# A feed-forward input made of seven products: PSUM evictions, weight buffers and adding DMAs rearranged

## The chip, the cores and the metric

The kernel runs on one core of one Trainium2 chip. The metric is the device time of one execution in microseconds; lower is better. The time before is the median of three runs.

## The reference, cut to what matters

The kernel computes one inference step of one decoder layer for 512 prompt tokens and 8 sampled tokens, 520 columns in all. Only the last part of the layer is touched: an RMSNorm, the feed-forward input (two projections of width 2816 from 1024), SwiGLU, and the projection back.

```python
    h = x + (m @ w_o).astype(x.dtype)

    hn = rms_norm(h, norm_ffn_g)
    f_gate, f_up = jnp.split(hn @ w_ffn_in, 2, axis=-1)
    h = h + ((jax.nn.silu(f_gate) * f_up) @ w_ffn_down).astype(x.dtype)
```

Every matrix product is wanted at float32 accuracy. The kernel splits each float32 operand into a high and a low float32r part and adds three products of parts (high x high, high x low, low x high).

## The kernel before

The layer is computed with features on the 128 partitions and the 520 tokens along the free dimension, in two halves of 260 columns, L and R. Stages follow each other in the program: retention heads, gMLP, the merge, the `w_o` projection (L826 to L835), and then the feed-forward part, which begins at about 778 us of the profiled execution. The program is written in the Tile layer: instructions are recorded in program order, and a planner (`schedule_with_timeline_sim=True`, L1012) orders them on each engine by program order and by modelled times of when their data and a free buffer are there. The hardware then works through each engine's queue in that order. GpSimd and SP also issue the DMAs, in their queues.

The feed-forward input has 22 output blocks of 128 gate columns and 128 up columns. One call of `ffn_in(i)` (a pair below) makes one such block for both halves of the tokens. Instead of eight block products (two halves of the contraction, gate and up, two halves of tokens) it uses seven, by sums in the manner of Strassen and Winograd. The names are those of the code:

- `sum_weights` (L727 to L755) makes the seven weight operands of a pair. `ab` are two plain blocks, loaded by SP (L743). `s13` is a pair of sums: SP loads one block twice (L740), and an adding DMA of GpSimd's queue adds two other blocks (L741). `s24` is made from `s13` and `ab` by two VectorE additions (L750, L751). Each of these three tiles of 128x1024 is split (`split`, L88 on ScalarE for the high part, L91 on VectorE for the low part). The seventh operand, d, is loaded by a GpSimd DMA that converts it into `wdh` (L746); ScalarE writes its negative into `wdl` (L747), and a second, adding GpSimd DMA makes that the low part (L748).
- `wtile` (L74 to L79) hands out the buffers. For `wraw` it goes round five (three in pool `wp`, two in `wq`), for `whi` and `wlo` four each. `weights`, which loads the other projections, uses the same buffers.
- `sum_acts` (L757 to L803) makes the seven operands from the normalised input once, from a tile `xsum`.
- `seven` (L805 to L822) runs the seven products in the order of `ORDER`, each of 12 matmuls of 260 columns. They add into three PSUM banks: a, s2, s3, d into bank 0, s1 and s4 into bank 1, b into bank 2. Banks 0 and 1 are one tile of the pool `psm` (two buffers), bank 2 is one of `aux` (four buffers). After each product `seen` reads what is wanted of the partial sum.
- `seen` in `ffn_in` (L855 to L876) does these evictions: L857 (a), L859 (b), L861 (s1), L863 (s2), L865 (s3), L867 (s4), then on GpSimd the product of both halves of `fa` with `rstd` (L870), Silu on ScalarE (L871), the product of the right halves on GpSimd (L872) and, after d, the product of the left half straight from bank 0 on VectorE (L874).

The pairs come in batches of 10, 8 and 4; after each batch a down projection (`ffn_down`, L890) uses 8, 8 and 6 of the finished blocks. The planner mixes matmuls of neighbouring pairs, and of the down projection with pairs.

Of the kernel before, what the change touches and what calls it, by code (L numbers as in the profile page):

```python
# [7 lines left out]
F32 = mybir.dt.float32  # L8
F32R = mybir.dt.float32r
# [4 lines left out]
P = 128  # L14
# [27 lines left out]
def step_kernel(ctx: ExitStack, tc: tile.TileContext, io):  # L42
# [35 lines left out]
    def wtile(kind, dt=F32R):  # L78

        pools = wpools[kind]  # L80
        pool = pools[wturn[kind] % len(pools)]
        wturn[kind] += 1
        return pool.tile([P, 8 * P], dt, name=kind, tag=kind, bufs=pools.count(pool))

    def split(hi, lo, src, hi_eng=None, lo_eng=None):

        if hi_eng is None:
            nc.scalar.copy(out=hi, in_=src)  # L88
        else:
            hi_eng.tensor_copy(out=hi, in_=src)  # L90
        (lo_eng or nc.vector).tensor_tensor(out=lo, in0=src, in1=hi.bitcast(F32), op=ALU.subtract)  # L91
# [53 lines left out]
    def row_rstd(out, ps, width):  # L145

        y, v, t = (stile(f"rr_{x}") for x in "yvt")
        for f in range(2):
            nc.vector.tensor_scalar(
                out=v[:, f * HT : (f + 1) * HT], in0=ps[f][:, 0:HT], scalar1=1.0 / width, scalar2=EPS,  # L150
                op0=ALU.mult, op1=ALU.add,
            )
        root = nc.scalar.activation(out=y, in_=v, func=AF.Abs_reciprocal_sqrt)
        nc.vector.scalar_tensor_tensor(out=t, in0=y, scalar=-0.5, in1=y, op0=ALU.mult, op1=ALU.mult)
        nc.vector.tensor_tensor(out=t, in0=t, in1=v, op=ALU.mult)
        nc.vector.scalar_tensor_tensor(out=out, in0=t, scalar=1.5, in1=y, op0=ALU.add, op1=ALU.mult)
        return root
# [561 lines left out]

    ORDER = "a b s1 s2 s3 s4 d".split()
    MEETS = dict(a=0, s1=1, b=2, d=6, s4=3, s3=4, s2=5)

    fp = ctx.enter_context(tc.tile_pool(name="fp", bufs=1))
# [1 line left out]
    def sum_weights(src):  # L727

        def block(t):
            return t.rearrange("p (a b) -> p a b", a=2)  # L730

        def both(t):
            hi, lo = wtile("whi"), wtile("wlo")
            split(hi, lo, t)
            hi, lo = block(hi), block(lo)
            return [(hi[:, i], lo[:, i]) for i in range(2)]

        s13 = block(wtile("wraw", F32))
        for i in range(2):
            nc.sync.dma_start(out=s13[:, i], in_=src[:, 0])  # L740
        nc.gpsimd.dma_start(out=s13, in_=src[:, 1:3], accum_op=ALU.add)  # L741
        ab = block(wtile("wraw", F32))
        nc.sync.dma_start(out=ab, in_=src[:, 2:4])  # L743
        dh = wq.tile([P, 4 * P], F32R, name="wdh")
        dl = wq.tile([P, 4 * P], F32R, name="wdl")
        nc.gpsimd.dma_start(out=dh, in_=src[:, 1])  # L746
        nc.scalar.activation(out=dl, in_=dh.bitcast(F32), func=AF.Copy, scale=-1.0)  # L747
        nc.gpsimd.dma_start(out=dl, in_=src[:, 1], accum_op=ALU.add)  # L748
        s24 = block(wtile("wraw", F32))
        nc.vector.tensor_tensor(out=s24[:, 0], in0=s13[:, 0], in1=ab[:, 0], op=ALU.add)  # L750
        nc.vector.tensor_tensor(out=s24[:, 1], in0=s24[:, 0], in1=ab[:, 1], op=ALU.add)  # L751
        w = {"d": (dh, dl)}
        for names, t in (("a b", ab), ("s1 s3", s13), ("s2 s4", s24)):
            w |= dict(zip(names.split(), both(t.rearrange("p a b -> p (a b)"))))
        return w  # L755

    def sum_acts(fill, name, pairs):  # L757

        out = [[] for _ in range(7)]
        more = None  # L760
        for j in range(pairs):
            x = fp.tile([P, 7, HT], F32, name="xsum", bufs=1)
            fill(j, x)
            tt, stt = nc.vector.tensor_tensor, nc.vector.scalar_tensor_tensor
            tt(out=x[:, 4], in0=x[:, 3], in1=x[:, 1], op=ALU.subtract)
            tt(out=x[:, 1], in0=x[:, 0], in1=x[:, 1], op=ALU.subtract)
            stt(out=x[:, 5], in0=x[:, 3], scalar=-1.0, in1=x[:, 1], op0=ALU.mult, op1=ALU.subtract)
            stt(out=x[:, 6], in0=x[:, 5], scalar=-1.0, in1=x[:, 2], op0=ALU.mult, op1=ALU.subtract)

            def slots(t):  # L770
                return t.rearrange("p a (b c) -> p (a b) c", b=2)

            h, l = slots(pair(f"{name}h{j}")), slots(pair(f"{name}l{j}"))
            split(h, l, x[:, 0:4])
            for i in range(4):
                out[i].append((h[:, i], l[:, i]))

            if j % 2 == 0:
                more = [slots(pair(f"{name}m{j}{i}")) for i in range(3)]
            at = [(6 * k + 3 * (j % 2) + i) for k in range(2) for i in range(3)]  # L780
            at = [(more[n // 4], n % 4) for n in at]
            for k in range(2):
                i = 0
                while i < 3:
                    t, n = at[3 * k + i]
                    m = 1
                    while i + m < 3 and at[3 * k + i + m][0] is t:
                        m += 1
                    src = x[:, 4 + i : 4 + i + m]
                    if k == 0:  # L790
                        nc.scalar.copy(out=t[:, n : n + m], in_=src)
                    else:
                        for ii in range(i, i + m):
                            th, nh = at[ii]
                            tl, nl = at[3 + ii]
                            nc.vector.tensor_tensor(
                                out=tl[:, nl], in0=x[:, 4 + ii], in1=th[:, nh].bitcast(F32), op=ALU.subtract
                            )
                    i += m
            for i in range(3):  # L800
                (th, nh), (tl, nl) = at[i], at[3 + i]
                out[4 + i].append((th[:, nh], tl[:, nl]))
        return out  # L803

    def seven(w, x, name, seen):  # L805

        ps = acc_psum(name)
        bank = [ps[:, 0, 0:HT], ps[:, 1, 0:HT], aux(f"{name}3")[:, 0:HT]]
        into = dict(a=0, b=2, s1=1, s2=0, s3=0, s4=1, d=0)
        begun = set()  # L810
        for s in ORDER:
            to = into[s]
            acts = x[MEETS[s]]
            for k, (xh, xl) in enumerate(acts):
                sl = slice(k * P, (k + 1) * P)
                for n, (ww, xx) in enumerate(((w[s][0], xh), (w[s][0], xl), (w[s][1], xh))):
                    nc.tensor.matmul(  # L817
                        bank[to], ww[:, sl], xx, start=to not in begun,
                        stop=k == len(acts) - 1 and n == 2, skip_group_check=True,
                    )  # L820
                    begun.add(to)
            seen(s, bank)  # L822

    hs = fp.tile([P, KT, T], F32, name="hs")
# [19 lines left out]
    hx = sum_acts(fill_h, "hx", KT // 2)  # L844


    rstd = const.tile([P, T], F32, name="rstd")
    act = []
    L, R = slice(0, HT), slice(HT, T)

    def ffn_in(i):

        a, b = ttile("fa"), ttile("fb")

        def seen(s, bank):  # L855
            if s == "a":
                nc.scalar.copy(out=a[:, L], in_=bank[0])  # L857
            elif s == "b":
                nc.vector.tensor_tensor(out=a[:, L], in0=a[:, L], in1=bank[2], op=ALU.add)  # L859
            elif s == "s1":  # L860
                nc.scalar.activation(out=b[:, R], in_=bank[1], func=AF.Copy, scale=-1.0)  # L861
            elif s == "s2":
                nc.scalar.copy(out=a[:, R], in_=bank[0])  # L863
            elif s == "s3":
                nc.vector.tensor_tensor(out=b[:, R], in0=b[:, R], in1=bank[0], op=ALU.subtract)  # L865
            elif s == "s4":
                nc.vector.tensor_tensor(out=a[:, R], in0=a[:, R], in1=bank[1], op=ALU.add)  # L867
                if i == 0:
                    row_rstd(rstd, row_sums(sq), D)
                nc.gpsimd.tensor_tensor(out=a, in0=a, in1=rstd, op=ALU.mult)  # L870
                nc.scalar.activation(out=a, in_=a, func=AF.Silu)  # L871
                nc.gpsimd.tensor_tensor(out=b[:, R], in0=a[:, R], in1=b[:, R], op=ALU.mult)  # L872
            else:
                nc.vector.scalar_tensor_tensor(  # L874
                    out=b[:, L], in0=bank[0], scalar=-1.0, in1=a[:, L], op0=ALU.mult, op1=ALU.mult
                )  # L876

        seven(sum_weights(io["w_ffn_in"][i].rearrange("p (s c) -> p s c", s=4)), hx, "ps_f", seen)
        pr = pair(f"act{i}")
        split(pr[:, 0, :], pr[:, 1, :], b)  # L880
        act.append(pr)
# [143 lines left out]
```

## Time and profile before

| | us |
|---|---|
| runs | 1202.44, 1203.23, 1206.78; median 1203.23 |
| profiled execution | 1210.7 |
| its span in the trace | 1209.0 |
| TensorE busy | 1137.1 (94%) |
| VectorE busy | 761.1 (63%) |
| ScalarE busy | 500.2 (41%) |
| GpSimd busy | 313.0 (26%) |

Durations and waits are taken from the one profiled execution. In the rows PE is TensorE, PEld its weight loads, DVE VectorE, ACT ScalarE, POOL GpSimd and SP the engine that issues most loads. An output is written as out<-in by the program's tile names, with buffer numbers left out, so `wraw` stands for the tiles of `s13`, `ab` and `s24` alike. PEclk is the granted TensorE clock as a share of full speed. A wait names the instruction that came last before it.

### The profile page before, as it was taken

Reading aid. Unit: us, or ns where it says so; the run is one execution under the profiler, and the core shown is the slowest. Engines: PE = TensorE matmul, PEld = TensorE weight load, DVE = VectorE, ACT = ScalarE, POOL = GpSimd, SP = SyncE. Lnnn points to the kernel's source line nnn. Section 1 sums busy time; section 2 is a strip of 40 time slices with the busy share of each in tenths; the row PEclk is TensorE's granted clock in tenths of the full one; section 3 lists DMA queues with packets and bytes.
Section 4 is the critical chain, followed back from the end, with each engine's and each line's share of the span. In section 5 each row is a group of like instructions: output and inputs, shape, how many; then the busy total and the mean of one; then the engine's idle time right before and its main releaser. Section 6 shows DMA issues by size and latency. Waiting matters only on the chain.

```text
span 1209.0 us, 21757 instructions
## 1 busy us (share of the span) xinstructions
PE 1137.1 (94%) x8978; PEld 1113.8 (92%) x8978; DVE 761.1 (63%) x1192; ACT 500.2 (41%) x790; POOL 313.0 (26%) x286
## 2 busy tenths in 40 slices
PE   7999999999999998999999999988889978899994
PEld 7998999999999998999999999988879978899893
DVE  7778647965886687466434476966655545565654
ACT  4365346443633554232323333654443234432442
POOL 7213201310140031003111222223324223333343
PEclk9999999999999999998998999998999989999998
DMA  7267237533843475222222225447655457554502
GB/s 266 90 224 262 98 122 259 195 123 111 297 158 121 149 275 165 88 80 71 88 88 71 88 88 158 106 116 171 154 161 148 100 136 162 161 147 99 149 28 70
DMA packets 57603, 170.60 MB, mean 141 GB/s; under 512 B 6768, under 2 KB 9216, under 8 KB 57496
## 3 DMA queue, kind: packets, MB, share of 16 engines
q1 hardware_dynamic: 40320, 118.76, 29.9%
q0 software_dynamic: 17184, 50.45, 16.1%
q8 instruction: 70, 1.15, 0.4%
q14 instruction: 29, 0.24, 0.1%
HBM read 148.09 MB, written 21.10 MB: 140 GB/s over the span
## 4 chain that ended last, share of the span: by engine, by line
PE 63%; DMA 14%; DVE 11%; issue 4%; ACT 4%; POOL 1%; DVEq 0%; SPq 0%; POOLq 0%; ACTq 0%
PE ps_f L817 10%; PE ps_fd L109 10%; PE ps_ro L109 8%; DMA wraw<-in_w_ffn_in 7%; PE ps_v L109 5%; PE ps_gu L109 4%; PE ps_ar L109 4%; PE ps_gm L109 4%; PE ps_ag L109 3%; DVE wlo L91 3%; PE k L109 3%; PE ps_gv L109 3%; PE ps_wo L109 3%; DMA wdh<-in_w_ffn_in 3%; DMA S<-in_st 2%
## 5 line engine op out<-in xcount | busy, mean ns | idle before, releaser
L88 ACT CAST whi<-wraw 128x1024 fp32r<-128x1024 f32 (+3 forms) x205 | 210.2, 1027 | 350.7 <-issue 75.8
L91 DVE TENSOR_TENSOR wlo<-wraw,whi 128x1024 fp32r<-128x1024 f32 (+3 forms) x205 | 293.3, 1433 | 75.1 <-ACT whi L88 68.2
L817 PE MATMUL ps_f<-hxh,whi 128*128 128x260 f32 x352 | 104.4, 299 | 28.4 <-DVE fb L874 19.1
L109 PE MATMUL ps_fd<-act,whi 128*128 128x260 f32 x704 | 113.5, 282 | 1.0 <-DVE fb L874 0.8
L817 PE MATMUL ps_f<-hxl,whi 128*128 128x260 f32 x352 | 103.2, 294 | 1.8 <-DVE hxl L91 1.8
L817 PE MATMUL ps_f<-hxh,wlo 128*128 128x260 f32 x352 | 102.0, 294 | 0.0
L817 PEld LDWEIGHTS ps_f<-hxh,whi 128*128 128x128 f32 x352 | 69.4, 198 | 32.1 <-DVE fb L874 21.0
L109 PEld LDWEIGHTS ps_fd<-act,whi 128*128 128x128 f32 x704 | 96.7, 188 | 1.5 <-DVE fb L874 1.0
L109 PE MATMUL ps_g<-xg,whi 128*128 128x260 f32 x512 | 82.4, 283 | 0.0
L109 PE MATMUL ps_ro<-gated,whi 128*128 128x260 f32 x512 | 82.3, 283 | 0.0
L109 PE MATMUL ps_v<-xg,whi 128*128 128x260 f32 x512 | 82.1, 282 | 0.0
L817 PEld LDWEIGHTS ps_f<-hxl,whi 128*128 128x128 f32 x352 | 70.3, 200 | 2.0 <-DVE hxl L91 2.0
L109 PE MATMUL ps_fd<-act,wlo 128*128 128x260 f32 x352 | 71.9, 283 | 0.0
L109 PEld LDWEIGHTS ps_ro<-gated,whi 128*128 128x128 f32 x512 | 70.5, 188 | 0.5
L817 PEld LDWEIGHTS ps_f<-hxh,wlo 128*128 128x128 f32 x352 | 69.8, 200 | 0.4 <-DVE wlo L91 0.4
L109 PEld LDWEIGHTS ps_v<-xg,whi 128*128 128x128 f32 x512 | 70.0, 188 | 0.0
L109 PEld LDWEIGHTS ps_g<-xg,whi 128*128 128x128 f32 x512 | 69.7, 188 | 0.0
L817 PE MATMUL ps_f<-hxm,whi 128*128 128x260 f32 x352 | 68.2, 291 | 0.2 <-ACT fb L861 0.2
L453 POOL DMA_DIRECT2D out_rss<-S x32 | 17.0, 532 | 191.7 <-DVE S L452 191.7
L451 ACT ACTIVATE kv<-qkb,vs 128x256 f32<-128x256 f32 x128 | 54.1, 498 | 26.3 <-DMA qkb<-qks 20.7
L817 PEld LDWEIGHTS ps_f<-hxm,whi 128*128 128x128 f32 x352 | 56.9, 197 | 0.4 <-ACT fb L861 0.4
L456 DVE SCALAR_TENSOR_TENSOR junk<-S,qkb 128x256 f32<-128x256 f32 x128 | 53.9, 421 | 2.3
(268 smaller groups left out, 2835.7 us busy)
## 6 DMA issues: line engine op xcount, KB each, us to landing
wraw<-in_w_in SPq DMA_DIRECT2D x78, 512.0 KB, 3.5
S<-in_st SPq DMA_DIRECT2D x32, 512.0 KB, 4.6
out_rss<-S POOLq DMA_DIRECT2D x32, 512.0 KB, 5.0
wraw<-in_w_ffn_in SPq DMA_DIRECT2D x44, 256.0 KB, 4.0
wraw<-in_w_ffn_in POOLq DMA_DIRECT2D x22, 512.0 KB, 6.3
wraw<-in_w_ffn_in SPq DMA_DIRECT2D x22, 512.0 KB, 5.1
qkb<-qks POOLq DMA_DIRECT2D x16, 512.0 KB, 5.2
wraw<-in_w_ret_o SPq DMA_DIRECT2D x16, 512.0 KB, 3.5
```

Of the source, the lines that this page charges most:

```text
L88: nc.scalar.copy(out=hi, in_=src)
L91: (lo_eng or nc.vector).tensor_tensor(out=lo, in0=src, in1=hi.bitcast(F32), op=ALU.subtract)
L109: nc.tensor.matmul((ps[f] if isinstance(ps, list) else ps[:, f])[:, 0:HT], a, x[:, k, f * HT : (f + 1) * HT], start=first and n == 0, stop ...
L451: nc.scalar.activation(out=kv[:, j, :], in_=kb, func=AF.Copy, scale=vs[:, j, b : b + 1])
L453: nc.gpsimd.dma_start(out=io["rss"][b, h].rearrange("p (j d) -> p j d", j=NC), in_=S)
L456: nc.vector.scalar_tensor_tensor(out=junk, in0=S[:, j, :], scalar=1.0, in1=qb, op0=ALU.mult, op1=ALU.mult, accum_out=os_[:, j, b : b + 1],)
L817: nc.tensor.matmul(bank[to], ww[:, sl], xx, start=to not in begun, stop=k == len(acts) - 1 and n == 2, skip_group_check=True,)
```

## The change

The order of products becomes a, s1, b, s2, s3, s4, d. Product b is added onto product a: ScalarE copies bank 0 into bank 2 after a, and b adds there without starting anew. Evictions: b's bank is multiplied by `rstd` on its way out (left half), GpSimd multiplies only the right half by `rstd`, d's bank is copied out negated by ScalarE, and one GpSimd product over both halves follows. `rstd` is made after product a of the first pair. Four matmuls that nobody reads (`ps_mark`) stand ahead of the pairs.

For the weights: `s13` has the three buffers of `wp`, `ab` the two of `wq`, `s24` and the new plain tile `d` one each. d is loaded by SP as float32 and split like the others, last in the pair; the two GpSimd DMAs for it and the negated copy are gone. `ab` and `s13` are split ahead of the two sums. The tile `xsum` becomes two tiles of the large pool, and the last three operands of each part are split one by one.

```diff
-    ORDER = "a b s1 s2 s3 s4 d".split()
+    ORDER = "a s1 b s2 s3 s4 d".split()
...
-        s13 = block(wtile("wraw", F32))
+        s13 = block(wp.tile([P, 8 * P], F32, name="s13", tag="wraw", bufs=3))
         for i in range(2):
             nc.sync.dma_start(out=s13[:, i], in_=src[:, 0])
         nc.gpsimd.dma_start(out=s13, in_=src[:, 1:3], accum_op=ALU.add)
-        ab = block(wtile("wraw", F32))
+        ab = block(wq.tile([P, 8 * P], F32, name="ab", tag="wraw", bufs=2))
         nc.sync.dma_start(out=ab, in_=src[:, 2:4])
-        dh = wq.tile([P, 4 * P], F32R, name="wdh")
-        dl = wq.tile([P, 4 * P], F32R, name="wdl")
-        nc.gpsimd.dma_start(out=dh, in_=src[:, 1])
-        nc.scalar.activation(out=dl, in_=dh.bitcast(F32), func=AF.Copy, scale=-1.0)
-        nc.gpsimd.dma_start(out=dl, in_=src[:, 1], accum_op=ALU.add)
-        s24 = block(wtile("wraw", F32))
+        d = fp.tile([P, 4 * P], F32, name="d", bufs=1)
+        nc.sync.dma_start(out=d, in_=src[:, 1])
+        w = dict(zip("a b".split(), both(ab.rearrange("p a b -> p (a b)"))))
+        w |= dict(zip("s1 s3".split(), both(s13.rearrange("p a b -> p (a b)"))))
+        s24 = block(fp.tile([P, 8 * P], F32, name="s24", bufs=1))
         nc.vector.tensor_tensor(out=s24[:, 0], in0=s13[:, 0], in1=ab[:, 0], op=ALU.add)
         nc.vector.tensor_tensor(out=s24[:, 1], in0=s24[:, 0], in1=ab[:, 1], op=ALU.add)
-        w = {"d": (dh, dl)}
-        for names, t in (("a b", ab), ("s1 s3", s13), ("s2 s4", s24)):
-            w |= dict(zip(names.split(), both(t.rearrange("p a b -> p (a b)"))))
+        w |= dict(zip("s2 s4".split(), both(s24.rearrange("p a b -> p (a b)"))))
+        w["d"] = tuple(wq.tile([P, 4 * P], F32R, name=f"wd{x}") for x in "hl")
+        split(*w["d"], d)
         return w
...
-            x = fp.tile([P, 7, HT], F32, name="xsum", bufs=1)
-            fill(j, x)
+            x0, x1 = (wide("xsum").rearrange("p a (b c) -> p (a b) c", b=2) for _ in range(2))
+            x = [x0[:, i] for i in range(4)] + [x1[:, i] for i in range(3)]
+            fill(j, x0)
...
             for i in range(3):
                 (th, nh), (tl, nl) = at[i], at[3 + i]
+                split(th[:, nh], tl[:, nl], x[4 + i])
                 out[4 + i].append((th[:, nh], tl[:, nl]))
...
-        begun = set()
+        begun = {2}
...
+            if s == "a":
+                nc.scalar.copy(out=bank[2], in_=bank[0])
             seen(s, bank)
...
+    for _ in range(4):
+        nc.tensor.matmul(aux("ps_mark")[:, 0:HT], ones_r, hx[0][0][0], start=True, stop=True)
...
             if s == "a":
-                nc.scalar.copy(out=a[:, L], in_=bank[0])
+                if i == 0:
+                    row_rstd(rstd, row_sums(sq), D)
             elif s == "b":
-                nc.vector.tensor_tensor(out=a[:, L], in0=a[:, L], in1=bank[2], op=ALU.add)
+                nc.vector.tensor_tensor(out=a[:, L], in0=bank[2], in1=rstd[:, L], op=ALU.mult)
...
                 nc.vector.tensor_tensor(out=a[:, R], in0=a[:, R], in1=bank[1], op=ALU.add)
-                if i == 0:
-                    row_rstd(rstd, row_sums(sq), D)
-                nc.gpsimd.tensor_tensor(out=a, in0=a, in1=rstd, op=ALU.mult)
+                nc.gpsimd.tensor_tensor(out=a[:, R], in0=a[:, R], in1=rstd[:, R], op=ALU.mult)
                 nc.scalar.activation(out=a, in_=a, func=AF.Silu)
-                nc.gpsimd.tensor_tensor(out=b[:, R], in0=a[:, R], in1=b[:, R], op=ALU.mult)
             else:
-                nc.vector.scalar_tensor_tensor(
-                    out=b[:, L], in0=bank[0], scalar=-1.0, in1=a[:, L], op0=ALU.mult, op1=ALU.mult
-                )
+                nc.scalar.activation(out=b[:, L], in_=bank[0], func=AF.Copy, scale=-1.0)
+                nc.gpsimd.tensor_tensor(out=b, in0=a, in1=b, op=ALU.mult)
```

## Rows read from the trace of the kernel before

**Rows 1.** The page, busy time, share of the span and instructions of each engine.

```profile
PE 1137.1 (94%) x8978; PEld 1113.8 (92%) x8978; DVE 761.1 (63%) x1192; ACT 500.2 (41%) x790; POOL 313.0 (26%) x286
```

**Rows 2.** Busy time by stretch: its bounds, length, then each engine's busy time (instructions).

```profile
core 0: us, PE busy (x) PEld busy (x) DVE busy (x) ACT busy (x) POOL busy (x), PEclk, DMA share, GB/s
778.00:1157.00 379.00, 339.01 (x2657) 332.93 (x2655) 219.86 (x265) 151.92 (x222) 121.84 (x119) 0.96 0.57 139
800.00:908.00 108.00, 90.00 (x689) 87.49 (x688) 64.04 (x80) 49.50 (x77) 37.89 (x41) 0.95 0.67 165
908.00:952.00 44.00, 44.00 (x371) 44.00 (x370) 23.60 (x24) 11.79 (x14) 16.46 (x14) 1.00 0.55 129
```

**Rows 3.** The chain that ended last, second down projection: start, us, what.

```profile
1066.99 40.15 PE ps_fd L109 x336
```

**Rows 4.** TensorE's waits, 778 to 1157 us: total us, times, longest.

```profile
PE ps_f L817 <- DVE fb L874: 19.1, 9, 3.6
PE ps_f L817 <- ACT fa L857: 8.0, 3, 4.1
PE ps_f L817 <- DVE fa L867: 7.9, 4, 3.5
```

**Rows 5.** Timeline, VectorE and TensorE at 881 us: start, us, what, [idle before <-releaser].

```profile
881.14 0.69 DVE L750 TENSOR_TENSOR wraw<-wraw 128x512 f32<-128x512 f32 x1 [5.37 <-DMA wraw<-in_w_ffn_in]
881.75 0.42 DVE L867 TENSOR_TENSOR fa<-fa,ps_f 128x260 f32<-128x260 f32 x1
...
882.22 0.51 PE L817 MATMUL ps_f<-hxm,wdh 128*128 128x260 f32 x2 [3.31 <-DVE fa L867]
```

**Rows 6.** Timeline, ScalarE and TensorE at 899 us.

```profile
899.30 0.63 ACT L747 ACTIVATE wdl<-wdh 128x512 fp32r<-128x512 f32 x1 [3.84 <-DMA wdh<-in_w_ffn_in]
899.84 1.03 ACT L88 CAST whi<-wraw 128x1024 fp32r<-128x1024 f32 x1
900.77 0.37 ACT L857 COPY fa<-ps_f 128x260 f32<-128x260 f32 x1
...
901.19 0.39 PE L817 MATMUL ps_f<-hxh,whi 128*128 128x260 f32 x1 [2.58 <-ACT fa L857]
```

**Rows 7.** Timeline, GpSimd at 830 us.

```profile
830.65 0.85 POOL L741 DMA_DIRECT2D wraw<-in_w_ffn_in  x1 [8.16 <-DMA wraw<-in_w_ffn_in]
831.22 1.59 POOL L870 TENSOR_TENSOR fa<-fa,rstd 128x520 f32<-128x520 f32 x1
```

**Rows 8.** Waits of the other engines, 778 to 1157 us: total us, times, longest.

```profile
POOL wraw L741 <- DMA wraw<-in_w_ffn_in: 76.4, 12, 18.9
...
DVE wraw L750 <- DMA wraw<-in_w_ffn_in: 38.0, 15, 5.4
...
ACT fa L871 <- POOL fa L870: 32.2, 14, 4.9
...
ACT wdl L747 <- DMA wdh<-in_w_ffn_in: 30.9, 13, 4.6
...
ACT fa L857 <- PE ps_f L817: 3.0, 4, 0.8
```

**Rows 9.** The page, DMA issues: count, KB each, median us to landing.

```profile
wraw<-in_w_ffn_in SPq DMA_DIRECT2D x44, 256.0 KB, 4.0
wraw<-in_w_ffn_in POOLq DMA_DIRECT2D x22, 512.0 KB, 6.3
...
wdh<-in_w_ffn_in POOLq DMA_DIRECT2D x22, 256.0 KB, 4.9
```

**Rows 10.** Instruction groups, shapes apart, 778 to 1157 us: busy us, mean ns | idle.

```profile
L870 POOL TENSOR_TENSOR fa<-fa,rstd 128x520 f32<-128x520 f32 x22 | 34.3, 1559 | 50.2 <-DVE fa L867 49.9
...
L750 DVE TENSOR_TENSOR wraw<-wraw 128x512 f32<-128x512 f32 x20 | 17.1, 855 | 38.1 <-DMA wraw<-in_w_ffn_in 38.0
...
L863 ACT COPY fa<-ps_f 128x260 f32<-128x260 f32 x22 | 8.3, 375 | 14.6 <-PE ps_f L817 14.5
```

**Rows 11.** Waits of SP's DMA queue, whole span: total us, times, longest.

```profile
SPq L740 <- DVE wlo L91: 141.4, 20, 13.1
```

More of the change, by code (lines that the diff above doesn't have):

```diff
@@ L761, in sum_acts @@
         for j in range(pairs):
-            x = fp.tile([P, 7, HT], F32, name="xsum", bufs=1)
-            fill(j, x)
+            x0, x1 = (wide("xsum").rearrange("p a (b c) -> p (a b) c", b=2) for _ in range(2))
+            x = [x0[:, i] for i in range(4)] + [x1[:, i] for i in range(3)]
+            fill(j, x0)
             tt, stt = nc.vector.tensor_tensor, nc.vector.scalar_tensor_tensor
[L765 to L768, printed above, removed]
+            tt(out=x[4], in0=x[3], in1=x[1], op=ALU.subtract)
+            tt(out=x[1], in0=x[0], in1=x[1], op=ALU.subtract)
+            stt(out=x[5], in0=x[3], scalar=-1.0, in1=x[1], op0=ALU.mult, op1=ALU.subtract)
+            stt(out=x[6], in0=x[5], scalar=-1.0, in1=x[2], op0=ALU.mult, op1=ALU.subtract)
             def slots(t):
@@ L773, in sum_acts @@
             h, l = slots(pair(f"{name}h{j}")), slots(pair(f"{name}l{j}"))
-            split(h, l, x[:, 0:4])
+            split(h, l, x0)
             for i in range(4):
@@ L779, in sum_acts @@
                 more = [slots(pair(f"{name}m{j}{i}")) for i in range(3)]
[L780 to L797, printed above, removed]
-                            )
-                    i += m
+            at = [(more[n // 4], n % 4) for n in (6 * k + 3 * (j % 2) + i for k in range(2) for i in range(3))]
             for i in range(3):
                 (th, nh), (tl, nl) = at[i], at[3 + i]
+                split(th[:, nh], tl[:, nl], x[4 + i])
                 out[4 + i].append((th[:, nh], tl[:, nl]))
@@ L867, in seen @@
                 nc.vector.tensor_tensor(out=a[:, R], in0=a[:, R], in1=bank[1], op=ALU.add)
-                if i == 0:
-                    row_rstd(rstd, row_sums(sq), D)
-                nc.gpsimd.tensor_tensor(out=a, in0=a, in1=rstd, op=ALU.mult)
+                nc.gpsimd.tensor_tensor(out=a[:, R], in0=a[:, R], in1=rstd[:, R], op=ALU.mult)
                 nc.scalar.activation(out=a, in_=a, func=AF.Silu)
-                nc.gpsimd.tensor_tensor(out=b[:, R], in0=a[:, R], in1=b[:, R], op=ALU.mult)
             else:
-                nc.vector.scalar_tensor_tensor(
-                    out=b[:, L], in0=bank[0], scalar=-1.0, in1=a[:, L], op0=ALU.mult, op1=ALU.mult
-                )
+                nc.scalar.activation(out=b[:, L], in_=bank[0], func=AF.Copy, scale=-1.0)
+                nc.gpsimd.tensor_tensor(out=b, in0=a, in1=b, op=ALU.mult)
         seven(sum_weights(io["w_ffn_in"][i].rearrange("p (s c) -> p s c", s=4)), hx, "ps_f", seen)
```

## The prediction

> **What bounds the kernel now.** I read the page first, then the busy time of stretches, then the waits of the stretch that loses time, and last the queues behind those waits. TensorE is busy 94% of the span [rows 1], so only time in which it stands or runs slowly can be won. The change touches the stage from the first `ps_f` matmul (778 us) to the last (1157 us) and the few microseconds before it. That stage holds 2657 matmuls in 379.0 us [rows 2]. What one costs when nothing is late is seen in a down projection inside it: 336 matmuls in 40.15 us, 0.1195 us each [rows 3]. So 2657 x 0.1195 = 317.5 us are work and 61.5 us are lost. The loss is in the pairs (a pair is one call of `ffn_in`), not in the down projections: 800 to 908 us, nearly all pairs, has 689 matmuls at a granted clock of 0.95, where 908 to 952, nearly all down projection, is busy throughout at 1.00 [rows 2].
>
> TensorE's own waits in the stage are mostly three: for `fb` (L874) 19.1 us, for `fa` (L857) 8.0, for `fa` (L867) 7.9 [rows 4], together 35.0. The smaller ones bring that to 39.2 us; the other 61.5 - 39.2 = 22.3 us are the lower clock after a wait and the small restarts, 0.57 us for each us waited.
>
> Those three lines are only evictions out of the banks, of about 0.4 us. What is to be seen is why they were late: each engine works through its queue in order, and the planner that wrote the queues (modelled times, L1012) put a weight step ahead of the eviction whose data had not come. VectorE stood 5.37 us at L750, the first sum of weight blocks, for a DMA; the eviction L867 is right behind it, and TensorE waited 3.31 us for that [rows 5]. I followed the 13 waits of 19.1 and 7.9 us: in 11 of them L750 is the late step, in two (0.5 us each) nothing is. ScalarE stood 3.84 us at L747, the negated copy of `wdh`, for its DMA; the copy L857 is behind it and TensorE waited 2.58 us [rows 6]; the three waits of 8.0 us are all of this kind. In two of the 11 GpSimd was late first: its adding DMA L741 stood 8.16 us for the plain loads, and the product with `rstd` (L870) behind it held Silu and then L874 [rows 7]. In total L750 waited 38.0 us for DMAs, L747 30.9, L741 76.4 [rows 8].
>
> **The change part by part.** *The d block (L744 to L748).* Gone are two DMA issues on GpSimd and L747's wait. The old load wrote straight into `wdh`, so it could not start before TensorE had left that buffer; the new one goes to a buffer of its own, on SP, and is split last in its pair. The nearest row for its landing is SP's 256 KB load, 4.0 us, against 4.9 for the old one [rows 9]; its buffer is free again after the split before it, about one pair earlier (84 x 0.1195 = 10.0 us). So I take the whole of this wait as gone: 8.0 x 1.57 = 12.6 us. Ends: 0 (the split waits as L747 did) and 12.6. It costs VectorE 22 subtractions of 128x512; a two-input one of that shape has a mean of 0.855 us, or 0.69 undisturbed [rows 5, 10], so 15 to 19 us more on an engine that is busy 219.9 of 379.0 us [rows 2]. I cost that at nothing; if the cover fails it shows as a later eviction, as below.
>
> *Buffers by kind.* `s13` gets three buffers, `ab` two, the sums and d one each, in place of five shared. Today SP waits 141.4 us in 20 waits for a split (L91) to free a buffer before it can load s13 [rows 11]. From that load to the sum is a chain of landing 4.0, issue on GpSimd 0.85, landing 6.3 [rows 7, 9]: 11 us, longer than the pair's 10.0. With three buffers the load of a pair may start once the pair three before it is summed, some 30 us ahead, and the split of ab and s13 no longer stands behind the sum. What goes is L750's part: 19.1 + 7.9 = 27.0, with its clock 27.0 x 1.57 = 42.4 us. I take 60% of it, 25.4 us. Two of the 11 waits (3.25 + 3.64 of 25.9 us) began on GpSimd, and L741 is still placed there by modelled landings; the rest I leave for the first pairs after a down projection. Ends: 0 and 42.4. Next late is then GpSimd's product behind L741.
>
> *Evictions.* The last bank is copied out by ScalarE at once, not multiplied by Silu's result, so the buffer that the next pairs wait for no longer needs GpSimd's product (1.56 us mean) and Silu after s4 [rows 10]. It is behind Silu in ScalarE's queue if the planner puts it so; ScalarE waited 32.2 us there for GpSimd [rows 8]. That gain lies inside the 25.4. ScalarE gets 22 copies of 0.38 us, 8 us on an engine busy 151.9 of 379.0 [rows 2, 10]. GpSimd's elements are the same: 520 and 260 become 260 and 520.
>
> *The new wait.* Product b now adds onto the copy of a in the third bank, so TensorE needs that copy after one product of cover (s1, 12 x 0.1195 = 1.43 us). Queued behind it are the pair's whole rest, since TensorE is in order. The copy takes 0.375 us [rows 10]; but today its counterpart L857 waited for TensorE in only 4 of 22 pairs [rows 8], so in 18 it stood behind something, mostly casts of 1.0 us [rows 6]. One cast ahead: 1.0 + 0.375 is within the cover. Two: 2.1 + 0.375 + 0.15 = 2.6, so 1.2 us a pair. Ends 0 and 22 x 1.2 = 26.4 us; I take 0.2 a pair, 4.4 us, nearer to the one cast that rows 6 shows.
>
> *The rest.* Four `ps_mark` matmuls: 4 x 0.12 = 0.5 us. The Trainium skill, PSUM — Partial Sum Buffer, Summary: rules for kernel authors, speaks against the third bank: a sum seeded by ScalarE should start from 0, as engine writes don't set the bits by which a matmul adds. By it these matmuls are what makes the addition hold, and the 0.5 us is its price; no run here shows the bits. `xsum` moves to two tiles of the large pool and six casts of summed inputs become twelve: at most 0.4 us each on the last block, against L750 gone from between its steps; I take 0. `rstd` is made at a of the first pair; its matmuls run early already.
>
> Sum: -12.6 - 25.4 + 4.4 + 0.5 = -33.1 us. Against the profiled execution's 1210.7 us that is 1177.6; its span is 1209.0, and the runs' median of 1203.2 gives 1170.1 us.
>
> **The rivals.** *GpSimd stays the blocker (0.20).* L741 is queued where the loads are modelled to land, and every product and Silu behind it waits; the 76.4 us of rows 8 speak for it, that most were idle time with no product behind speaks against. Only the d part is won: -12.6 + 4.9 = -7.7, 1195.5 us.
>
> *The wait only moves (0.12).* Single buffers for d and the sums hold SP's queue: a load of d that waits for a split keeps the next s13 behind it. Then both kinds of stall stay, less a little issue time on GpSimd, which is not on the path: gain about 5 us against the 4.9 added, 1203 us. The Trainium skill, DMA: Bandwidth & Descriptors, Issuing engines are not separate DMA queues, agrees with this case: a transfer moved to another engine's queue saves only the time to issue it. Its landing has rows of 4.0 against 4.9 us, so the d part would then be near 0.
>
> *Slower: the copy of a (0.12).* Two casts stand ahead of the copy in every pair, at the second step of TensorE's order: +26.4, and sums placed early again keep the 42.4. Then -12.6 + 26.4 + 0.5 = +14.3, 1217.5 us. It decides from about 2.9 us between the end of a and the end of its copy (1.43 of cover + 33/22): from there the whole gain is gone. The 18 of 22 late copies speak for it, the room on ScalarE (152 of 379 us) against.
>
> **How the numbers follow.** The forecast has 0.56, own range 1150 to 1188: below it only the whole 42.4 and no new wait (1203.2 - 55 = 1148). The range 1150 to 1206 takes in the first two rivals and leaves out the slower one and the lowest end, about 0.17. A measurement of this kernel tells 0.5%, 6 us, from no change. Faster is the forecast and the first rival, 0.76; same the second, 0.12; slower the third, 0.12.
>
> **What would show it.** Right: L750 and the d split wait under 10 us each for DMAs in the stage; SP's waits for s13 fall from 141 us; TensorE's waits from 39 to under 20 and the clock of 800 to 900 us at 0.98 or more. Wrong: ScalarE's copy into the third bank tops TensorE's waits (slower rival); Silu's wait for GpSimd stays near 32 us (first); the d split waits near 31 us (second).

## The result and the profile after

The changed kernel takes 1160.3 us (median of 4 runs, 1157.44 to 1161.14) against 1203.4 before: 0.9633 of the time, 95% interval 0.9608 to 0.9658, so 43.1 us faster by the medians, where 33.1 were forecast. The profiled executions are 1210.7 and 1161.1 us, their spans 1209.0 and 1159.4. Of that difference of 49.6 about 5 us are most likely not the change's: in before's profiled execution, which is itself 7 us longer than the median, the first `ps_f` matmul comes at 778 us, in that of after at 773. The lead is there already at the first matmul of the stage before `w_o` (`ps_gm`, 687 against 681 us; 677 to 682 in the other kernels below, whichever weight path they have). What the change touches shrank from 379 us [rows 2] to 333.

Line numbers of after: L741 is the adding DMA as before, L749 and L750 the two sums, L799 the products, L805 the copy of bank 0 into bank 2, L848 b's eviction, L854 s3's, L856 s4's, L857 the half product with `rstd`, L858 Silu, L860 the negated copy of d's bank, L861 the last product. The tiles that all were `wraw` are now `s` (s13 and s24), `ab` and `d`.

Busy time of each engine over the span, from the page of after (compare [rows 1]):

```profile
PE 1120.1 (97%) x8982; PEld 1098.7 (95%) x8982; DVE 763.2 (66%) x1192; ACT 507.7 (44%) x818; POOL 292.6 (25%) x242
```

Busy time by stretch of after, columns as in [rows 2]: the stage, steady pairs, the start of the stage, the rest of it.

```profile
773.00:1106.00 333.00, 325.27 (x2653) 320.97 (x2651) 222.29 (x264) 159.07 (x245) 98.69 (x77) 0.99 0.52 139
800.00:880.00 80.00, 79.81 (x662) 79.19 (x661) 59.19 (x76) 48.19 (x79) 26.06 (x20) 1.00 0.61 166
773.00:791.00 18.00, 14.76 (x96) 13.86 (x95) 12.90 (x22) 10.44 (x18) 0.00 (x0) 0.81 0.24 65
791.00:1106.00 315.00, 310.52 (x2560) 307.11 (x2558) 209.39 (x243) 148.62 (x228) 98.69 (x77) 1.00 0.54 143
```

Steady pairs now run TensorE 79.81 of 80 us at a granted clock of 1.00; before it was 90.0 of 108 at 0.95 [rows 2]. With 0.1195 us a matmul [rows 3], the stage holds 2653 x 0.1195 = 317.0 us of work and loses 16.0, where it lost 61.5. That is 45.5 us won inside the stage. Of the 16.0 left, 18.0 - 96 x 0.1195 = 6.5 are lost in the first 18 us, at a granted clock of 0.81, TensorE's first waits for the input operands (`hxh`, `hxl` below) among them; the other 315 us lose 9.1.

TensorE's waits of after in the stage: who waited for whom, total us, times, longest.

```profile
PE ps_f L799 <- DVE fb L854: 1.6, 3, 0.5
PE ps_f L799 <- ACT hxh L88: 1.5, 1, 1.5
PE ps_fd L109 <- DVE fd L882: 1.3, 1, 1.3
PE ps_f L799 <- DVE hxl L91: 0.8, 1, 0.8
...
PE ps_f L799 <- ACT ps_f L805: 0.4, 2, 0.2
```

The 19.1, 8.0 and 7.9 us of [rows 4] are gone, and the new wait, for the copy into the third bank (L805), is 0.4 us. All of TensorE's waits for pairs and down projections (`ps_f` and `ps_fd`, 765 to 1160 us, so with the last down projection) come to 8.1 us here and to 39.1 before; below, "TensorE's waits" is always this sum. The waits of the engines that had stood in the way, same stretch:

```profile
POOL s L741 <- DMA s<-in_w_ffn_in: 33.8, 4, 20.5
...
ACT fa L858 <- POOL fa L857: 15.7, 20, 1.9
...
DVE s L749 <- DMA s<-in_w_ffn_in: 8.5, 1, 8.5
...
DVE s L749 <- DMA ab<-in_w_ffn_in: 4.1, 1, 4.1
```

VectorE's sum waits twice for a DMA, 12.6 us in all, where it waited 38.0 us in 15 waits [rows 8]; both lie in down projections, at 907 and 1041 us, and only the second costs TensorE anything, the 1.3 us for `fd` L882 above. ScalarE waits for no DMA of d any more, where it had 30.9 us [rows 8]. SP's queue still waits for a split to free the buffer of s13, and GpSimd's adding DMA (L741) for SP's loads, but TensorE now loses next to nothing by it; SP's row over the whole span, beside [rows 11]:

```profile
SPq L740 <- DVE wlo L91: 91.6, 22, 12.4
```

The timeline of after in a steady pair (start, us, what, and in brackets any idle time before it) shows what became of [rows 5]: the sum and the eviction behind it follow without a gap.

```profile
833.46 0.69 DVE L749 TENSOR_TENSOR s<-s,ab 128x512 f32<-128x512 f32 x1
...
834.12 0.43 DVE L848 TENSOR_TENSOR fa<-ps_f,rstd 128x260 f32<-128x260 f32 x1
```

### The profile page after: what moved, and what is told of

Its sections match the earlier page's. It is cut to its first block, busy times and chain, and to the rows that moved or that the text cites. A ratio compares the mean times of both kernels' runs of the same rounds, so it can differ in the third digit from the quotient of the medians.

```text
span 1159.4 us, 21723 instructions
## 1 busy us (share of the span) xinstructions
PE 1120.1 (97%) x8982; PEld 1098.7 (95%) x8982; DVE 763.2 (66%) x1192; ACT 507.7 (44%) x818; POOL 292.6 (25%) x242
## 4 chain that ended last, share of the span: by engine, by line
PE 77%; DVE 9%; DMA 4%; ACT 4%; issue 2%; POOL 1%; DVEq 0%; SPq 0%; ACTq 0%; POOLq 0%
PE ps_f L799 14%; PE ps_fd L109 10%; PE ps_ro L109 8%; PE ps_v L109 8%; PE ps_g L109 6%; PE ps_gu L109 4%; PE ps_ar L109 4%; PE ps_gm L109 4%; PE ps_gv L109 4%; PE ps_ag L109 3%; PE q L109 3%; PE k L109 3%; DVE wlo L91 2%; PE ps_o L469 2%; ACT whi L88 2%
## 5 line engine op out<-in xcount | busy, mean ns | idle before, releaser
L88 ACT CAST whi<-wraw 128x1024 fp32r<-128x1024 f32 (+3 forms) x139 | 141.3, 1018 | 278.5 <-issue 67.1
L91 DVE TENSOR_TENSOR wlo<-wraw,whi 128x1024 fp32r<-128x1024 f32 (+3 forms) x139 | 192.2, 1384 | 37.8 <-ACT whi L88 35.7
L799 PE MATMUL ps_f<-hxh,whi 128*128 128x260 f32 x352 | 101.3, 289 | 4.6 <-DVE fb L854 1.6
L799 PE MATMUL ps_f<-hxl,whi 128*128 128x260 f32 x352 | 100.2, 285 | 0.8 <-DVE hxl L91 0.8
L799 PE MATMUL ps_f<-hxh,wlo 128*128 128x260 f32 x352 | 99.8, 285 | 0.6 <-DVE wlo L91 0.6
L799 PEld LDWEIGHTS ps_f<-hxh,whi 128*128 128x128 f32 x352 | 67.1, 191 | 7.2 <-DVE fb L854 2.2
L91 DVE TENSOR_TENSOR wlo<-s,whi 128x1024 fp32r<-128x1024 f32 x44 | 61.7, 1403 | 14.9 <-ACT whi L88 14.4
L799 PEld LDWEIGHTS ps_f<-hxl,whi 128*128 128x128 f32 x352 | 67.2, 191 | 1.1 <-DVE hxl L91 1.1
L799 PEld LDWEIGHTS ps_f<-hxh,wlo 128*128 128x128 f32 x352 | 67.0, 191 | 0.8 <-DVE wlo L91 0.8
L799 PE MATMUL ps_f<-hxm,whi 128*128 128x260 f32 x352 | 65.2, 282 | 0.3 <-ACT fa L852 0.3
L88 ACT CAST whi<-s 128x1024 fp32r<-128x1024 f32 x44 | 46.1, 1048 | 37.8 <-PE ps_fd L109 20.3
```

The source lines that it names most:

```text
L799: nc.tensor.matmul(bank[to], ww[:, sl], xx, start=to not in begun, stop=k == len(acts) - 1 and n == 2, skip_group_check=True,)
```

## The experiments

Two theories were set against each other. The first is that of the prediction: the evictions were late because weight steps stood ahead of them in the queues of VectorE and ScalarE and waited for DMAs, and the DMAs were late because their loads waited for a buffer. The rival: the gain comes from the evictions themselves (the third bank, the earlier release of bank 0). All kernels below compute the whole layer. Each was timed in turn with the kernel before on the same chip; ratios are to that.

### The weight path alone

before, with after's `sum_weights`. It needs after's `sum_acts` too: the pool of the old `xsum` has no room for the new tiles beside it. ORDER, the three banks and the evictions are before's.

> The kernel before with the new weight path alone (own buffers by kind, d by SP and split last, ab and s13 split ahead of the sums) and xsum in the large pool, which makes the room for it; order and evictions as before. Theory 1 (the loss was weight steps waiting for DMAs in front of evictions): most of the 43 us are here, about 1172 us (1165 to 1180), TensorE's waits in the stage under 15 us. Theory 2 (the loss was that a bank is freed only after GpSimd's product and Silu): little is here, about 1195 us (1188 to 1203), and TensorE still waits about 20 us for fb.

1165.3 us, 0.968 [0.9656, 0.9703]: 38.5 us of the gain are here. TensorE's waits fall from 39.1 to 13.3 us; its two longest rows for the products (L847 is s3's eviction here) are

```profile
PE ps_f L799 <- DVE fb L847: 4.9, 4, 3.5
...
PE ps_f L799 <- ACT whi L88: 2.1, 1, 2.1
```

None of before's three rows is left, though the evictions are before's. The first theory holds for most of the gain. The longest wait left is of another kind:

```profile
806.94 0.88 POOL L741 DMA_DIRECT2D s<-in_w_ffn_in  x1 [5.58 <-DMA s<-in_w_ffn_in]
...
808.61 0.62 ACT L88 CAST act<-fb 128x520 fp32r<-128x520 f32 x1 [5.28 <-POOL fb L854]
...
809.27 0.70 DVE L91 TENSOR_TENSOR act<-fb,act 128x520 fp32r<-128x520 f32 x1 [5.21 <-ACT act L88]
809.88 0.42 DVE L847 TENSOR_TENSOR fb<-fb,ps_f 128x260 f32<-128x260 f32 x1
...
810.36 0.39 PE L799 MATMUL ps_f<-hxh,whi 128*128 128x260 f32 x1 [3.48 <-DVE fb L847]
```

GpSimd stood 5.58 us at its adding DMA for the plain loads; a product of the pair before (L854) is behind it, the split of that product waits for it on ScalarE and then on VectorE, and the eviction stands behind the split.

### The evictions alone

after, with before's `sum_weights`: third bank, new order and new evictions on the old weight path.

> The changed kernel with the weight path of before (five shared buffers, two GpSimd DMAs for d, sums ahead of the splits); order, third bank and plain evictions stay changed. Theory 1: about 1198 us (1190 to 1206), the VectorE sum still waits near 38 us for DMAs. Theory 2: about 1168 us (1160 to 1178), the bank is free early whatever the weights do.

1201.2 us, 0.9985 [0.9965, 1.0006]: no change that can be told. The waits, of TensorE and of those in its way (L855 is s3's eviction here, L806 the copy into bank 2):

```profile
DVE wraw L750 <- DMA wraw<-in_w_ffn_in: 52.5, 17, 7.2
...
ACT wdl L747 <- DMA wdh<-in_w_ffn_in: 32.5, 20, 3.2
...
PE ps_f L800 <- DVE fb L855: 23.7, 11, 5.0
...
PE ps_f L800 <- ACT ps_f L806: 10.3, 10, 3.4
```

The sum and the negated copy stand as long as before, or longer, and TensorE's waits come to 40.2 us against 39.1. What is new is the last row: the copy into bank 2 is itself late, behind ScalarE's negated copy. So the rival falls as the cause of the gain.

### d as before, the rest as after

```diff
-        d = fp.tile([P, 4 * P], F32, name="d", bufs=1)
-        nc.sync.dma_start(out=d, in_=src[:, 1])
+        dh = wq.tile([P, 4 * P], F32R, name="wdh")
+        dl = wq.tile([P, 4 * P], F32R, name="wdl")
+        nc.gpsimd.dma_start(out=dh, in_=src[:, 1])
+        nc.scalar.activation(out=dl, in_=dh.bitcast(F32), func=AF.Copy, scale=-1.0)
+        nc.gpsimd.dma_start(out=dl, in_=src[:, 1], accum_op=ALU.add)
...
-        w["d"] = tuple(wq.tile([P, 4 * P], F32R, name=f"wd{x}") for x in "hl")
-        split(*w["d"], d)
+        w["d"] = (dh, dl)
```

> The changed kernel with d loaded as before: two GpSimd DMAs straight into the split buffers and the negated copy on ScalarE between them. Theory 1: ScalarE waits for d again, 8 to 13 us in the pairs and about 3 us where the first two loads are issued in the gMLP stage: 1174 us (1168 to 1179). Theory 2: the evictions no longer depend on it, 1162 us (1159 to 1166).

1196.3 us, 0.9925 [0.9901, 0.995]: the old d path alone gives back 36 us of the 43, some two and a half times what was expected. Its waits:

```profile
ACT wdl L747 <- DMA wdh<-in_w_ffn_in: 38.3, 20, 3.9
...
PE ps_f L801 <- ACT ps_f L807: 22.8, 10, 4.4
```

One of them in the timeline at 812 us:

```profile
811.75 0.63 ACT L747 ACTIVATE wdl<-wdh 128x512 fp32r<-128x512 f32 x1 [3.65 <-DMA wdh<-in_w_ffn_in]
812.29 0.37 ACT L807 COPY ps_f<-ps_f 128x260 f32<-128x260 f32 x1
...
812.71 0.39 PE L801 MATMUL ps_f<-hxh,whi 128*128 128x260 f32 x1 [3.97 <-ACT ps_f L807]
```

ScalarE stands 3.65 us for the DMA of d. The copy of bank 0 into bank 2 is right behind it, and now TensorE needs that copy for its next products: it stands 3.97 us. Eight waits make up 22.4 of that row's 22.8 us, and in all of them the copy is right behind L747. In before, the 30.9 us of L747's waits cost TensorE 8.0 us [rows 4, 8]; with the third bank 38.3 cost it 22.8.

### Shared buffers, the rest as after

```diff
-        s13 = block(wp.tile([P, 8 * P], F32, name="s13", tag="wraw", bufs=3))
+        s13 = block(wtile("wraw", F32))
...
-        ab = block(wq.tile([P, 8 * P], F32, name="ab", tag="wraw", bufs=2))
+        ab = block(wtile("wraw", F32))
...
-        s24 = block(fp.tile([P, 8 * P], F32, name="s24", bufs=1))
+        s24 = block(wtile("wraw", F32))
```

> The changed kernel with s13, ab and s24 taken from the five shared buffers as before; d by SP, splits ahead of the sums and evictions stay changed. Theory 1: the loads of s13 wait for a buffer again and the sum waits for the adding DMA: about 1183 us (1173 to 1195). Theory 2: 1162 us (1159 to 1167), with the sum's waits back but TensorE not held by them.

1193.3 us, 0.9904 [0.9883, 0.9924]: this alone gives back 33 us. The sum waits again, and TensorE with it:

```profile
DVE wraw L749 <- DMA wraw<-in_w_ffn_in: 48.1, 15, 6.9
...
PE ps_f L799 <- DVE fb L854: 25.0, 11, 5.7
```

At 825 us it is the pattern of [rows 5] once more: three weight steps of VectorE stand between the late data and the eviction.

```profile
824.75 0.69 DVE L749 TENSOR_TENSOR wraw<-wraw 128x512 f32<-128x512 f32 x1 [3.42 <-DMA wraw<-in_w_ffn_in]
...
825.48 0.69 DVE L750 TENSOR_TENSOR wraw<-wraw 128x512 f32<-128x512 f32 x1
826.08 0.68 DVE L91 TENSOR_TENSOR wdl<-d,wdh 128x512 fp32r<-128x512 f32 x1
...
826.68 0.42 DVE L854 TENSOR_TENSOR fb<-fb,ps_f 128x260 f32<-128x260 f32 x1
...
827.16 0.39 PE L799 MATMUL ps_f<-hxh,whi 128*128 128x260 f32 x1 [2.01 <-DVE fb L854]
```

So undoing either part costs nearly all of the gain. Two readings were open: on the old evictions the parts might add (each worth what the prediction gave it), or either stall alone might cover the other. Two kernels put one part alone on before.

### Own buffers alone, on before

before, with the three buffer lines above the other way round, and with after's `sum_acts` and after's order of splits; d and the evictions stay before's.

> The kernel before (its order, evictions and d path) with own buffers for s13, ab and s24, their splits ahead of the sums, and xsum in the large pool. Adding theory (the two stalls have prices of their own, as the prediction summed them): 1203 - 25 = 1178 us (1170 to 1185). Covering theory (a pair that is held by one stall gives the other's transfer time to land, so that either of them alone costs nearly as much as both): 1190 to 1203 us, with ScalarE's wait for d above the 31 us of before and TensorE's waits near 25 us.

1188.9 us, 0.9866 [0.9826, 0.9906]: 16 us, between the ranges of the two theories. TensorE's waits are 28.5 us. The rows that matter:

```profile
ACT wdl L747 <- DMA wdh<-in_w_ffn_in: 39.2, 18, 8.1
...
PE ps_f L801 <- ACT fa L841: 8.3, 5, 2.7
PE ps_f L801 <- ACT whi L88: 7.8, 5, 2.4
...
DVE s L752 <- DMA s<-in_w_ffn_in: 7.8, 1, 7.8
DVE s L752 <- DMA ab<-in_w_ffn_in: 5.8, 1, 5.8
```

The sum's stall is down to two waits, 13.6 us, both in down projections, as own buffers should do. But the stall of d, which had cost TensorE 8.0 us in before, costs more now: the row for L841 (copy of a, 8.3 us), 5.6 of the 7.8 us for weights cast late (`whi` L88) and 2.1 us for the eviction of s1 (L845) are ScalarE's work behind L747, 16 us in all.

### d's own buffer alone, on before

before, with after's d path and after's `sum_acts` and order of splits; `s13`, `ab` and `s24` share the five buffers.

> The kernel before (its order, evictions and five shared buffers) with d in a buffer of its own, loaded by SP and split last, the splits of ab and s13 ahead of the sums, and xsum in the large pool. Adding theory: 1203 - 13 = 1190 us (1186 to 1194). Covering theory: 1193 to 1203 us, with the sum's wait for DMAs above the 38 us of before.

1179.9 us, 0.9779 [0.9764, 0.9794]: 26.6 us by the ratio, better than either theory's number. TensorE's waits are 21.9 us (L856 is d's eviction here, L849 s4's).

```profile
DVE wraw L749 <- DMA wraw<-in_w_ffn_in: 33.3, 16, 6.0
...
PE ps_f L799 <- DVE fb L856: 15.1, 9, 3.8
...
PE ps_f L799 <- DVE fa L849: 3.8, 3, 3.5
```

The 8.0 us that TensorE lost to d's stall are gone, as forecast. But of the 27.0 us behind the sum [rows 4] only 18.9 are left (15.1 + 3.8), so d's path had a hand in these too. A reason that the rows allow: GpSimd no longer carries two issues for d with their waits ahead of L741 (in before's stage it stood 54.2 us at the second of them, L748, for ScalarE's negated copy). Since this kernel also has the ab and s13 splits ahead of the sums, the two were not told apart.

With these six and the two kernels themselves, all eight combinations are there. The first number is the ratio times 1203.4 less 1203.4, in us; the second, TensorE's waits. All but before have after's `sum_acts`, and all but before and the evictions alone after's order of splits. Neither was put on before by itself; the evictions alone, with `sum_acts`, won nothing, and in after the order of splits is worth nothing (below).

| weight path | old evictions | new evictions |
|---|---|---|
| old | 0, 39.1 | -1.8, 40.2 |
| own buffers, old d | -16.1, 28.5 | -9.0, 33.5 |
| own d, shared buffers | -26.6, 21.9 | -11.6, 32.2 |
| both | -38.5, 13.3 | -44.2, 8.1 |

On the old evictions the parts nearly add: 16.1 + 26.6 = 42.7 against 38.5. On the new ones either stall covers the other almost wholly: 9.0 and 11.6 alone, 44.2 together. The new evictions are worth 5.7 us where nothing is late, nothing on the old path, and cost 7 and 15 us where one stall is left (the 7 is not clear of the noise: 0.9866 [0.9826, 0.9906] and 0.9925 [0.9901, 0.995] overlap a little). For d the reason is the copy in ScalarE's queue shown above. For the shared buffers the sum's wait is itself longer under the new evictions (48.1 against 33.3 us), and the late eviction stands behind three or four weight steps in VectorE's queue where it stood behind one or two; why the planner's order brings that about stays open.

### One more buffer, or its own buffer?

Two kernels keep the old form of a part and give it one buffer more. First after with `s13` and `ab` taken in turn from the five shared ones, and only `s24` on its own (the two upper hunks of the shared-buffer diff):

> The changed kernel with s13 and ab taken in turn from the five shared buffers, and only the sums in a buffer of their own. Theory (five buffers for two loaded tiles, in place of five for three, are what lets the loads start early): 1158 to 1167 us. Rival (a set for each kind is what counts): 1178 to 1195 us, the sum's wait for DMAs over 25 us.

1159.4 us, 0.961 [0.9595, 0.9625]: the same as after. Its row for the sum, two waits in place of 15:

```profile
DVE s L749 <- DMA wraw<-in_w_ffn_in: 9.4, 2, 4.7
```

"By kind" does nothing, then: five buffers for two loaded tiles a pair, in place of five for three tiles, is what counts. Second, after with the old d path (GpSimd's two DMAs and the negated copy), but three buffers for `wdh`:

```diff
-        dh = wq.tile([P, 4 * P], F32R, name="wdh")
+        dh = fp.tile([P, 4 * P], F32R, name="wdh", bufs=3)
```

(shown against the kernel with the old d above)

> The changed kernel with d loaded as before by two GpSimd DMAs and the negated copy between them, but with three buffers for the high part in place of two. Theory (the load of d came late because it wrote into a buffer that TensorE had to leave first): 1160 to 1170 us, ScalarE's wait for that load under 12 us. Rival (the chain of DMA, copy and adding DMA through two queues is itself too slow): 1185 to 1197 us.

1159.7 us, 0.9622 [0.9595, 0.9648]: again the same as after, with no wait of ScalarE for `wdh` in the stage. One buffer declaration turns 1196.3 into 1159.7. With the other buffers in place, neither the adding DMA for d, nor GpSimd's queue, nor the negated copy had been the trouble.

### What else was changed

d's plain load on GpSimd's queue in place of SP's (`nc.gpsimd.dma_start(out=d, in_=src[:, 1])`):

> The changed kernel with the plain load of d issued on GpSimd's queue instead of SP's; its own buffer, the split on ScalarE and VectorE and all else stay. Theory (the own buffer, loaded long before the split, is what takes the wait away): 1160 to 1168 us, and ScalarE waits under 10 us for d. Rival (GpSimd's queue was what held the d block up, behind the adding DMA and the products): 1180 to 1195 us, ScalarE's wait for d back at 20 to 35 us.

1158.3 us, 0.96 [0.9553, 0.9646]: no difference from after. The load lands as soon from either queue, 3.7 us here against 3.6 in after:

```profile
d<-in_w_ffn_in POOLq DMA_DIRECT2D x22, 256.0 KB, 3.7
```

The Trainium skill, DMA: Bandwidth & Descriptors, Issuing engines are not separate DMA queues, says that DMAs run on the same 16 DMA engines whichever engine started them; this run agrees. The 4.9 us of the converting load [rows 9], which the prediction set against SP's 4.0 there, were then not the queue's.

The two sums recorded ahead of the splits of `ab` and `s13`, as before the change:

> The changed kernel with the two sums recorded ahead of the splits of ab and s13, as before. Theory (with the loads early, the place of the sum no longer matters): 1158 to 1167 us. Rival (the sum standing ahead of the splits is what held VectorE): 1175 to 1190 us, and the sum waits over 25 us for DMAs in the stage.

1160.1 us, 0.9613 [0.9559, 0.9667]: with the loads early, the place of the splits does nothing.

d's bank left by VectorE's product with Silu's result, as before the change, with GpSimd's product on the right half only:

> The changed kernel with d's bank read as before, multiplied by the left half of Silu's result on VectorE, so that the bank is freed only after GpSimd's product and Silu. Theory (with the weights on time nobody needs the bank that soon): 1160 to 1167 us. Rival (freeing the bank early is worth what TensorE waited for fb): 1175 to 1185 us, with about 15 us of TensorE's waits for that eviction.

1160.5 us, 0.9618 [0.9571, 0.9666]: bank 0's earlier release is worth nothing once the weights are in time.

`ORDER = "a b s1 s2 s3 s4 d"`, so that b adds onto the copy of a with no product of the same pair between:

> The changed kernel with b right after a in the order of products, so that the copy of a into the third bank has no product of its own pair as cover. Theory (the copy is on the path as soon as its cover is gone): at least 0.375 + 0.15 us a pair and up to 1.2 more where a cast stands ahead: 1171 to 1190 us. Rival (the planner puts products of the neighbouring pair in between): 1158 to 1166 us.

1159.0 us, 0.9604 [0.9557, 0.9651], and TensorE's wait for the copy is

```profile
PE ps_f L799 <- ACT ps_f L805: 0.4, 2, 0.2
```

the same as in after. The cover for that copy is not s1: the planner puts products of the neighbouring pair between (at 846.9 to 848.3 us, for one, s3 of the pair before).

## Why the prediction was right, and where it was not

*The cause* was right. Weight steps waiting for late DMAs held the evictions behind them; with the old weight path the new evictions are worth 1.8 us, which can't be told from nothing, and the new weight path alone is worth 38.5. The factor by which a wait becomes time (1.57) held too: in the table, 16.1/10.6, 26.6/17.2, 38.5/25.8 and 44.2/31.0 are 1.5, 1.5, 1.5 and 1.4.

*The d block* was mis-sized: 12.6 us, given as its upper end, against 26.6 alone on before and 36 when undone in after. The step that failed is "8.0 x 1.57": I put each of TensorE's waits down to the engine that was last late in it, and took that as the whole price of the stall. Alone, the part took away 17.2 us of waits: the 8.0, 8.1 of those that I had booked under the sum, and 1.1 of small ones. Of these the row for a cast (`whi` L88, 1.3 us in before) had stood behind L747 too.

*Buffers by kind* was given 25.4 between 0 and 42.4. Alone on before it brings 16.1, since the stall of d then costs more elsewhere; undone in after it costs 33. I left 40% for GpSimd and the first pairs after a down projection. That remainder went to neither: Silu's wait for GpSimd fell from 32.2 us [rows 8] to 15.7, none over 1.9 us.

*The sum* of the two, 38.0, came near the weight path's 38.5 because one term was too small by 14.0 and the other too large by 9.3, with 4.2 covered between them. The total was better than its terms, and that is luck.

*The new wait* was the other miss: 4.4 us taken, 0 to 26.4 given (the 0.15 in the case of two casts has no row: in [rows 5, 6] a matmul follows the end of its eviction by 0.05), 0.4 measured. The cover was reckoned as one product, s1; the order of the queue holds other pairs' products there too, and b right behind a costs nothing. That, with the evictions' 5.7 us where I had booked their gain inside the buffers' term, is most of the 10.0 us between 33.1 and 43.1. Which part of the evictions brings the 5.7 is not settled; the order of b and d's eviction do not, and the intervals of 0.968 and 0.9633 overlap slightly. Of the 5.2 us by which TensorE's waits differ (13.3 and 8.1), 3.5 are the one wait at 810 us shown above. *ps_mark* at 0.5 us is too small to be seen here, and no run left it out.

*The rivals.* GpSimd as the next blocker: it still waits 33.8 us for plain loads, 20.5 of them at once, and with d's load in its queue 61.1 us, but in after no eviction stands behind that. With the old evictions one did (the 3.5 us at 810 us in the weight path alone), so this rival's mechanism is real, too small to decide. The wait that only moves: SP's queue still waits 91.6 us, far enough ahead. The slower copy of a did not come in after, but its mechanism is real: with the old d path the same copy is TensorE's longest wait, 22.8 us, and so the new evictions win nothing there.

*The signs* came as named but one: the sum waits 12.6 us for DMAs, not under 10, in two waits that lie outside the pairs. d's split waits for none, SP's waits fell from 141.4 to 91.6, TensorE's from 39.1 to 8.1, and the granted clock of 800 to 900 us is 1.00.

## What to carry to other kernels

Where a planner writes in-order queues from modelled times, look behind a late eviction for the step that stands ahead of it, and count that step's buffers: a load that can start one use earlier removed here what looked like an eviction problem, and one `bufs=3` was worth 36 us in the changed kernel. Don't price stalls by adding up the waits attributed to each: the same part made alone on the old kernel and undone in the new differed by a factor of two (16 against 33 us), since a stall that remains covers the other. A sum seeded in PSUM gives the bound engine one more copy to wait for, and so can make a remaining stall dearer (22.8 us against 8.0 here): give the loads their room first.

## What the runs showed of the hardware

Two things were unexpected. A copy from bank to bank by ScalarE costs no more than one from a bank to SBUF: 0.367 us a piece in after, where the copy of s2 to SBUF (L852) takes 0.373, and 0.375 in before [rows 10], for the same shape.

```profile
L852 ACT COPY fa<-ps_f 128x260 f32<-128x260 f32 x22 | 8.2, 373 | 12.6 <-PE ps_f L799 12.6
L805 ACT COPY ps_f<-ps_f 128x260 f32<-128x260 f32 x22 | 8.1, 367 | 3.4 <-PE ps_f L799 3.3
```

And the plain load of d is quicker to land than the converting one, 3.6 against 4.9 us [rows 9] at the same 256 KB (medians of 3.0 to 4.5 against 4.2 to 5.5 over all kernels here, and 3.7 for the plain one from GpSimd's queue), but as the kernel with three `wdh` buffers shows, where it took 5.2 us, that time was not what mattered. The page of after, DMA issues (count, KB each, median us to landing):

```profile
s<-in_w_ffn_in SPq DMA_DIRECT2D x44, 256.0 KB, 4.2
s<-in_w_ffn_in POOLq DMA_DIRECT2D x22, 512.0 KB, 6.2
...
d<-in_w_ffn_in SPq DMA_DIRECT2D x22, 256.0 KB, 3.6
```
